# Making the weight sums of a fast-product channel mixer in DRAM with adding transfers

## The chip, the cores and the metric

The kernel runs on one core of one Trainium2 chip. The core has a matrix engine (TensorE, "PE" in the profile; its weight loads are "PEld"), three engines for element work (VectorE "DVE", ScalarE "ACT", GpSimd "POOL") and SyncE ("SP"), which in this kernel only issues transfers. Sixteen DMA engines move the data. The metric is the device time of one execution in microseconds, the median of several runs.

## The reference: what is computed

The program is a small decoder trunk on 512 positions of width 1024, in float32: two layers, each a channel mixer, a token mixer and a second channel mixer, and a last norm. The first layer's token mixer is a latent attention (MLA), the second's a sparse attention (NSA). Only the channel mixers matter here:

```python
def swiglu(x, w_gate, w_up, w_down):
    return (jax.nn.silu(x @ w_gate) * (x @ w_up)) @ w_down

for i in range(DEPTH):
    h = h + 0.5 * swiglu(rmsnorm(h, ffn_norm_a[i]), ffn_a_w_gate[i], ffn_a_w_up[i], ffn_a_w_down[i])
    h = h + mixer_i(rmsnorm(h, mix_norm[i]))
    h = h + 0.5 * swiglu(rmsnorm(h, ffn_norm_b[i]), ffn_b_w_gate[i], ffn_b_w_up[i], ffn_b_w_down[i])
```

The hidden width is 2816, which is 22 blocks of 128. There are four channel mixers in all; in the order of the program they are numbered 1 to 4 here (`idx` 0 to 3 in the code). MLA runs between 1 and 2, NSA between 3 and 4, and 3 follows 2 directly.

## The kernel before, in words

**Tiles.** The residual stream lives in SBUF as eight tiles of 128 channels x 512 positions (`h`). Every operand of a matrix product is split into a high part, rounded to the fast matrix format, and the low remainder (`split`: ACT writes the high part with a copy, DVE subtracts it from the source to get the low part), and each product is done as three matrix instructions: high x high, high x low, low x high.

**A channel mixer** (`ffn`) goes through 22 hidden blocks `f`. For the first three (`PLAIN = 3`) gate and up products are done directly (`plain`). For `f` = 3 to 21 the two products, which share their input, are done as a 2x2 block product with seven products in place of eight (`product(j, ...)`, j = 1 to 7). The seven left operands come from the four quarters g0, g1 (gate weights, two halves of the input channels) and u0, u1 (up weights): g0, g1, u1 unchanged, and the four sums s1 = u0 + u1, u0 + g0, g0 + s1 and g1 + g0 + s1. `wsums` loads the gate slab (`rg`, tile tag `wr`, 512 KB) and the up slab (`ru`, 512 KB) on SP's queue, makes the four sums on DVE in place, and splits all seven operands on ACT and DVE. The 12 matrix instructions of one product take about 1.36 us, and the products of a block run in the order 1, 7, 6, 2, 5, 4, 3. Products 1, 6 and 5 add up in one PSUM bank (`x`, tile `px`), 7 and 4 in another (`q`, tile `pq`); between them ACT copies the bank out (lines 554, 556, 558, 561). So product 5 may only start when the copy of line 558 is done, and that copy waits for product 6; only product 2 lies between.

**Down products** lag behind: after the seven products of block `f` stand two or three `unit`s, each 18 matrix instructions for one 128-channel piece of the output over three finished hidden blocks. A unit loads its weights (`wdr`, 192 KB, two buffers) on SP's queue, ACT and DVE split them (`wd`), and DVE adds the result to `h` (line 468).

**What sets the order.** The program is written as above, and a scheduler that works with modelled costs then decides the order of the instructions on each engine and of the transfers on SP's queue. Each engine takes its own instructions in that order and waits at the head when an operand is not there; so does SP with the transfers it issues, and their data then goes through one queue, `q1`. Loads run far ahead of use where buffers allow: the up slab has three buffers and is loaded about two and a half blocks before its products, the gate slab two buffers, the unit weights two. POOL takes part only at the norms (line 289, sums of squares) and in the token mixers.

Of the kernel before, what the change touches and what calls it, by code (L numbers as in the profile page):

```python
# [11 lines left out]
F32 = mybir.dt.float32  # L12
# [3 lines left out]
ALU = mybir.AluOpType  # L16
# [30 lines left out]
HS = S // 2  # L47
KP = KC // 2
PLAIN = 3
PAD = 16  # L50
TILES = 24
XC = P + 2
# [9 lines left out]
class Kern:  # L62
# [13 lines left out]
    def setup(self):  # L76
        nc, cp, a = self.nc, self.cp, self.a

        self.nw, self.odd, self.nq = 0, 0, 0
        self.first = self.wp.tile([P, 2048 + 3 * PAD], F32R, tag="w0", name="w")
        small = self.wp.tile([P, 80], F32, name="small")
        self.vtc_all = small
        self.vtc, self.small_sums, self.stc = small[:, :12], small[:, 12:16], small[:, 32:]
        self.sts, self.nst = [small[:, 12 + 3 * i : 15 + 3 * i] for i in range(6)], 0
        self.gains = cp.tile([P, 64], F32, name="gains")
        nc.scalar.dma_start(self.gains[:, :53], a["gains"])
        self.ident = cp.tile([P, P], F32, name="ident")
        nc.scalar.dma_start(self.ident, a["c_ident"])  # L90
        self.ones = cp.tile([P, P], F32R, name="ones")
        nc.vector.memset(f32v(self.ones), 1.0)
        warm = self.bank("o", "warm")
        for _ in range(10):
            nc.tensor.matmul(warm.rearrange("p (a n) -> p a n", n=P), self.ones, self.ones[:, None, :].to_broadcast([P, 4, P]), start=True, stop=True)
        nc.scalar.dma_start(self.gains[:, 53:59], a["c_rvalid"])
        tiny = self.gains[:, 59:64]
        nc.scalar.activation(tiny[:, 0:1], f32v(self.ones)[:, 0:1], AF.Copy)
        self.tiny = tiny

        self.ngains = cp.tile([P, 32], F32, name="ngains")
        for i, x in enumerate(FGAINS):
            nc.vector.tensor_scalar(self.ngains[:, 8 * i : 8 * i + 8], self.gains[:, GAINS[x] : GAINS[x] + 8], -1.0, None, op0=ALU.mult)
        self.h, self.ahead, self.softmax, self.turn, self.chain, self.chained, self.hi_pool = [], [], False, 0, None, False, False
        self.gated = None
        self.h = [self.hp.tile([P, S], F32, name=f"h{c}") for c in range(KC)]

    def begin(self):
# [232 lines left out]
    def wsums(self, idx, f):  # L341


        nc, fp, w_gu = self.nc, self.fp, self.a["w_gu"]
        if f == PLAIN:

            rg = fp.tile([P, 1024], F32, tag="fr", bufs=3, name="rg")
        else:
            rg = self.wp.tile([P, 1024], F32, tag="wr", bufs=2, name="wr")
        nc.sync.dma_start(rg, w_gu[idx, f, 0])  # L350
        ru = fp.tile([P, 1024], F32, tag="fr", bufs=3, name="ru")
        nc.sync.dma_start(ru, w_gu[idx, f, 1])
        s1 = fp.tile([P, S], F32, tag="s1", bufs=1, name="s1")
        g0, g1, u0, u1 = rg[:, :S], rg[:, S:], ru[:, :S], ru[:, S:]

        def split(src, pool, tag, bufs):
            n = src.shape[1]
            if pool is self.wp:
                hi, lo = self.wtiles("half")
            elif n == 1024:  # L360
                hi, lo = self.sum_tiles(n)
            else:
                hi = pool.tile([P, n], F32R, tag=tag[0], bufs=bufs, name="wh")
                lo = pool.tile([P, n + 2 * PAD], F32R, tag=tag[1], bufs=bufs, name="wl")[:, 2 * PAD :]
            with self.tc.issue_after(self.evicted.ins) if f == PLAIN + 1 else nullcontext():
                self.split(src, hi, lo)
            return [(hi[:, x : x + S].rearrange("p (k c) -> p k c", c=P), lo[:, x : x + S].rearrange("p (k c) -> p k c", c=P))
                    for x in range(0, n, S)]

        w = {}  # L370
        w[1], w[2] = split(rg, self.wp, None, 2)
        nc.vector.tensor_tensor(s1, u0, u1, op=ALU.add)
        nc.vector.tensor_tensor(u0, u0, g0, op=ALU.add)
        w[7], w[4] = split(ru, fp, ("fh", "fl"), 3)
        nc.vector.tensor_tensor(g0, g0, s1, op=ALU.add)
        nc.vector.tensor_tensor(g1, g1, g0, op=ALU.add)
        w[6], w[3] = split(rg, fp, ("fh", "fl"), 3)
        w[5], = split(s1, fp, ("sh", "sl"), 2)
        return w
# [36 lines left out]
    def third_slab(self, src):  # L416
# [4 lines left out]
            self.split(raw, *w)  # L421
        self.ahead.append([t.rearrange("p (a b) -> p a b", b=P) for t in w])

    def pad(self, pool, n, tag):
        pool.tile([P, n], F32, tag=tag, bufs=1, name=tag)

    def ffn(self, idx, gain_next, ap, tp):
        nc, a = self.nc, self.a
        self.scr, self.fp = (tp, "sq", 1), tp
        ah, al, ht, row = {}, {}, [], None  # L430
        self.pad(ap, 5 * PAD, "pad0")
        tg, tu, units = {}, {}, []
# [34 lines left out]
        def add(c, p):  # L467
            nc.vector.scalar_tensor_tensor(self.h[c], p, 0.5, self.h[c], op0=ALU.mult, op1=ALU.add)  # L468
# [72 lines left out]
        for f in range(PLAIN, NF):  # L541
# [25 lines left out]
            for work, tag in zip(todo, "oTS"):  # L567
                work(tag)
            act(f)
        if gain_next == "fin":  # L570

            hs, out = [self.parts(self.four(F32)) for _ in range(4)], []
# [961 lines left out]
```

## Time and profile before

| what | value |
|---|---|
| median of 3 runs | 1863.67 us (1863.41 to 1864.48) |
| the profiled execution's own time | 1862.05 us |
| its span, first to last instruction | 1860.3 us |
| granted TensorE clock | 0.999 |
| PE busy | 1845.7 us, 99% |
| PEld busy | 1763.4 us, 95% |
| DVE, ACT, POOL busy | 81%, 57%, 16% |
| DMA | 196.64 MB, mean 106 GB/s over the span |
| HBM read, written | 178.44 MB, 2.16 MB |

The page gives busy time for each engine, a strip of 40 slices, the DMA queues, the chain of work that ended last, the costliest groups of instructions, and the issues of transfers with the time from issue to landing. Matrix instructions are pipelined: one of 256 columns is listed with 276 ns, but in an undisturbed stretch the next starts 0.11 us later, so a short stall hides in the overlap and shows only in the distance between starts. A row of the timeline gives the start, the duration, the engine and line, the operation with its tiles, and in brackets how long the engine had stood idle and what ended that.

### The profile page before, as it was taken

The page shows a single profiled execution, that of the slowest core. Times are in us where ns is not written, and L with a number is a line of the kernel's source. Part 1 is how long each engine was busy: PE and PEld are TensorE (multiplying, and loading weights), DVE is VectorE, ACT ScalarE, POOL GpSimd, SP SyncE. Part 2 cuts the span into 40 slices and gives each one's busy share as a digit, 9 for nine tenths or more (in the row PEclk, how much of TensorE's full clock was granted, in tenths as well). Part 3 has the DMA queues.
Part 4 walks back from the last instruction along what each step waited for, and adds up shares of the span by engine and source line. Part 5 has one row for each costly group of instructions (what it writes and reads, how often), then busy time and mean ns, then how long its engine had stood idle before and what let it go on. Part 6 is the DMA issues. An engine that isn't in the chain of part 4 may idle for free.

```text
span 1860.3 us, 37031 instructions
## 1 busy us (share of the span) xinstructions
PE 1845.7 (99%) x14464; PEld 1763.4 (95%) x14464; DVE 1507.4 (81%) x2810; ACT 1064.5 (57%) x1997; POOL 296.7 (16%) x370
## 2 busy tenths in 40 slices
PE   9999999999999999999999999999999999999998
PEld 9999999888889999999999999988888889999997
DVE  8988886688779988886898888666878888888885
ACT  7555553567666555554655545446776865555554
POOL 0000000258830000001000000022666620000000
PEclk9999999999999999999999999999999999999999
DMA  6433331434433433322443332162433133433321
GB/s 238 132 108 103 103 92 48 117 105 103 114 123 112 119 103 109 110 73 72 138 118 110 109 106 81 45 183 82 108 108 103 40 118 116 121 104 107 103 78 69
DMA packets 84351, 196.64 MB, mean 106 GB/s; under 512 B 10944, under 2 KB 38464, under 8 KB 84176
## 3 DMA queue, kind: packets, MB, share of 16 engines
q1 hardware_dynamic: 81664, 191.34, 34.9%
q10 hardware_dynamic: 2512, 2.93, 0.5%
q8 instruction: 114, 1.87, 0.4%
q14 instruction: 61, 0.50, 0.1%
HBM read 178.44 MB, written 2.16 MB: 97 GB/s over the span
## 4 chain that ended last, share of the span: by engine, by line
PE 93%; DVE 3%; ACT 1%; issue 1%; POOL 1%; DMA 0%; ACTq 0%; POOLq 0%; DVEq 0%
PE pd L462 8%; PE pd L464 8%; PE pd L463 8%; PE px L386 6%; PE px L388 6%; PE px L387 5%; PE pg L386 4%; PE pg L388 4%; PE pg L387 4%; PE pq L386 4%; PE pq L388 4%; PE pq L387 4%; PE o L1337 2%; PE pt L1310 2%; PE po L197 2%; PE po L199 2%
## 5 line engine op out<-in xcount | busy, mean ns | idle before, releaser
L462 PE MATMUL pd<-ah,wd 128*128 128x256 f32 x1152 | 318.3, 276 | 0.0
L464 PE MATMUL pd<-ah,wd 128*128 128x256 f32 x1152 | 318.3, 276 | 0.0
L463 PE MATMUL pd<-al,wd 128*128 128x256 f32 x1152 | 318.3, 276 | 0.0
L289 POOL TENSOR_TENSOR s<-s,sq 128x512 f32<-128x512 f32 x38 | 54.7, 1441 | 1050.3 <-ACT sq L285 1050.3
L462 PEld LDWEIGHTS pd<-ah,wd 128*128 128x128 f32 x1152 | 216.3, 188 | 0.0
L464 PEld LDWEIGHTS pd<-ah,wd 128*128 128x128 f32 x1152 | 216.3, 188 | 0.0
L463 PEld LDWEIGHTS pd<-al,wd 128*128 128x128 f32 x1152 | 216.3, 188 | 0.0
L206 DVE TENSOR_TENSOR w<-wr,w 128x1024 fp32r<-128x1024 f32 x72 | 88.2, 1225 | 120.7 <-ACT w L205 120.4
L386 PE MATMUL px<-four,wh 128*128 128x256 f32 x608 | 168.4, 277 | 0.4 <-ACT wh L205 0.2
L388 PE MATMUL px<-four,wl 128*128 128x256 f32 x608 | 168.2, 277 | 0.2 <-DVE wl L206 0.2
L386 PE MATMUL pq<-four,wh 128*128 128x256 f32 x608 | 168.1, 276 | 0.2 <-ACT uq L556 0.2
L387 PE MATMUL px<-four,wh 128*128 128x256 f32 x608 | 168.0, 276 | 0.0
L388 PE MATMUL pq<-four,wl 128*128 128x256 f32 x608 | 167.9, 276 | 0.0
L387 PE MATMUL pq<-four,wh 128*128 128x256 f32 x608 | 167.9, 276 | 0.0
L468 DVE SCALAR_TENSOR_TENSOR h<-pd,h 128x512 f32<-128x512 f32 x216 | 148.3, 686 | 15.4 <-PE pd L464 15.2
L205 ACT ACTIVATE wd<-wdr 128x384 fp32r<-128x384 f32 x192 | 99.2, 519 | 103.8 <-issue 64.6
L176 ACT ACTIVATE w<-wr 128x1024 fp32r<-128x1024 f32 (+3 forms) x89 | 80.8, 908 | 87.5 <-PE pd L464 20.6
L206 DVE TENSOR_TENSOR wd<-wdr,wd 128x384 fp32r<-128x384 f32 x192 | 105.8, 553 | 20.1 <-ACT wd L205 20.0
L178 DVE TENSOR_TENSOR w<-wr,w 128x1024 fp32r<-128x1024 f32 (+3 forms) x75 | 78.3, 1044 | 50.0 <-ACT w L176 49.8
L728 ACT ACTIVATE p<-p,small 128x512 f32<-128x512 f32 (+2 forms) x192 | 106.9, 558 | 19.0 <-DVE small L727 15.3
L386 PEld LDWEIGHTS px<-four,wh 128*128 128x128 f32 x608 | 114.1, 188 | 1.0 <-ACT wh L205 0.4
L388 PEld LDWEIGHTS px<-four,wl 128*128 128x128 f32 x608 | 114.2, 188 | 0.6 <-DVE wl L206 0.6
(379 smaller groups left out, 6264.9 us busy)
## 6 DMA issues: line engine op xcount, KB each, us to landing
wr<-in_w_gu SPq DMA_DIRECT2D x93, 512.0 KB, 3.5
ru<-in_w_gu SPq DMA_DIRECT2D x76, 512.0 KB, 4.3
wdr<-in_w_down SPq DMA_DIRECT2D x192, 192.0 KB, 2.5
wr<-in_w_down SPq DMA_DIRECT2D x24, 256.0 KB, 2.6
wr<-in_mla_w_o SPq DMA_DIRECT2D x8, 512.0 KB, 3.4
th<-btab_d SPq DMA_DIRECT2D x16, 256.0 KB, 3.7
wr<-in_nsa_w_q SPq DMA_DIRECT2D x8, 512.0 KB, 3.8
wr<-in_nsa_w_o SPq DMA_DIRECT2D x8, 512.0 KB, 3.7
```

The lines of the kernel that those rows point to most:

```text
L176: self.copied = nc.scalar.activation(wh[:, m], raw[:, m], AF.Copy)
L178: nc.vector.tensor_tensor(wl[:, m], raw[:, m], f32v(wh[:, m]), op=ALU.subtract)
L205: nc.scalar.activation(hi, src, AF.Copy)
L206: (nc.gpsimd if pool else nc.vector).tensor_tensor(lo, src, f32v(hi), op=ALU.subtract)
L386: mm(out, wh[:, p], xh, start=first and p == 0, stop=False, skip_group_check=True)
L387: mm(out, wh[:, p], xl, start=False, stop=False, skip_group_check=True)
L388: mm(out, wl[:, p], xh, start=False, stop=last and p == KP - 1, skip_group_check=True)
L462: nc.tensor.matmul(o, wh, xh, start=k == b0 and x == 0, stop=False, skip_group_check=True)
L463: nc.tensor.matmul(o, wh, xl, start=False, stop=False, skip_group_check=True)
L464: last = nc.tensor.matmul(o, wl, xh, start=False, stop=k == b1 - 1, skip_group_check=True)
L468: nc.vector.scalar_tensor_tensor(self.h[c], p, 0.5, self.h[c], op0=ALU.mult, op1=ALU.add)
L728: nc.scalar.activation(p_sb[:, :n], p_sb[:, :n], AF.Exp, bias=nm, scale=-1.0, accum_out=sm)
```

## The change

For channel mixers 2, 3 and 4 the four sums of the blocks `f` = 3, 4, 5 and 6 are no longer made by DVE in those blocks. They are made in DRAM while the channel mixer before (1, 2 or 3) is running. For each such block a DRAM tile of 128 x 2560 floats is filled: SP issues one copy from DRAM to DRAM of both slabs (1,024 KB) and one of the second half of the up slab (256 KB), and POOL then issues four transfers of 256 KB each that add what they bring to what stands at the destination: u0 onto u1 (gives s1), g0 onto u0, s1 onto g0, and that sum onto g1. The third and fourth wait for the ones before them. The SP copies are tied to come after the load of the up slab of `f` = 9, 10, 11 or 12 of the running mixer.

In the block itself SP then loads, beside the plain gate slab, three pieces out of the DRAM tile: 512 KB into `ru` (as many bytes as before), 256 KB into `s1`, and 512 KB into a new tile `rp` with two buffers. The DVE sums fall away there; the splits stay. Mixer 1 and the blocks from 7 on are as before. The sums themselves are the same.

```diff
+SUMS = 3, 4, 5, 6
...
     def wsums(self, idx, f):
...
         nc.sync.dma_start(rg, w_gu[idx, f, 0])
         ru = fp.tile([P, 1024], F32, tag="fr", bufs=3, name="ru")
-        nc.sync.dma_start(ru, w_gu[idx, f, 1])
+        made = self.sums.pop((idx, f), None)
+        self.loaded = nc.sync.dma_start(ru, w_gu[idx, f, 1] if made is None else made[:, 1024:2048])
         s1 = fp.tile([P, S], F32, tag="s1", bufs=1, name="s1")
+        if made is not None:
+            rs = self.ap.tile([P, 1024], F32, tag="rp", bufs=2, name="rp")
+            nc.sync.dma_start(s1, made[:, 2048:])
+            nc.sync.dma_start(rs, made[:, :1024])
...
         w[1], w[2] = split(rg, self.wp, None, 2)
+        if made is not None:
+            w[7], w[4] = split(ru, fp, ("fh", "fl"), 3)
+            w[6], w[3] = split(rs, fp, ("fh", "fl"), 3)
+            w[5], = split(s1, fp, ("sh", "sl"), 2)
+            return w
         nc.vector.tensor_tensor(s1, u0, u1, op=ALU.add)
         nc.vector.tensor_tensor(u0, u0, g0, op=ALU.add)
         w[7], w[4] = split(ru, fp, ("fh", "fl"), 3)
         nc.vector.tensor_tensor(g0, g0, s1, op=ALU.add)
         nc.vector.tensor_tensor(g1, g1, g0, op=ALU.add)
...
+    def add_up(self, idx, f):
+
+        nc, src = self.nc, self.a["w_gu"][idx, f]
+        t = self.sums[idx, f] = self.dp.tile([P, 5 * S], F32, name=f"sums{idx}{f}")
+        with self.tc.issue_after(self.loaded.ins):
+            nc.sync.dma_start(t[:, :2048].rearrange("p (z n) -> p z n", z=2), src.rearrange("z p n -> p z n"))
+            nc.sync.dma_start(t[:, 2048:], src[1, :, S:])
+        add = partial(nc.gpsimd.dma_start, accum_op=ALU.add)
+        add(t[:, 2048:], src[1, :, :S])
+        add(t[:, 1024 : 1024 + S], src[0, :, :S])
+        add(t[:, :S], t[:, 2048:])
+        add(t[:, S:1024], t[:, :S])
...
     def ffn(self, idx, gain_next, ap, tp):
...
+        early = [partial(self.add_up, idx + 1, x) for x in SUMS] if idx < 3 else []
...
             act(f)
+            if early and f >= 3 * NG:
+                early.pop(0)()
```

**First place: SP's queue in mixer 2, around the start of its hidden block 7.** `wr` and `ru` are slabs of later blocks, `wdr` the weights of the block's units. Before:

```order
L350 DMA wr<-in_w_gu 128x1024
L352 DMA ru<-in_w_gu 128x1024
L474 DMA wdr<-in_w_down 128x384 x3
L350 DMA wr<-in_w_gu 128x1024
L352 DMA ru<-in_w_gu 128x1024
```

and now, with the DRAM tile of mixer 3's block 5 (`sums`):

```order
L351 DMA wr<-in_w_gu 128x1024
L354 DMA ru<-in_w_gu 128x1024
L440 DMA sums_9181<-in_w_gu 128x2x1024
L501 DMA wdr<-in_w_down 128x384 x2
L441 DMA sums_9181<-in_w_gu 128x512
L501 DMA wdr<-in_w_down 128x384
L351 DMA wr<-in_w_gu 128x1024
L354 DMA ru<-in_w_gu 128x1024
```

The 1,024 KB copy stands between the up slab and the first unit weights of the block, the 256 KB copy between the second and the third. In mixers 1, 2 and 3 together twelve such pairs are in the queue.

**Second place: ACT in the same block.** `wd<-wdr` is the split of the first unit weights, the other rows are the copies out of PSUM and the split of the next gate slab. Before:

```order
L554 ACTIVATE pg<-px 128x256
L205 ACTIVATE wd<-wdr 128x384
L556 ACTIVATE uq<-pq 128x256
L558 ACTIVATE uq<-px 128x256
L205 ACTIVATE w<-wr 128x1024
```

and now:

```order
L581 ACTIVATE pg<-px 128x256
L583 ACTIVATE uq<-pq 128x256
L206 ACTIVATE wd<-wdr 128x384
L585 ACTIVATE uq<-px 128x256
L206 ACTIVATE w<-wr 128x1024
```

The split of the unit weights has gone behind the first copy of `pq`, and still stands ahead of the second copy of `px`.

**Third place: SP's queue in mixer 2 while its blocks 3 to 5 run.** Here the made sums of mixer 2 are loaded: `ru` and `rp` of 512 KB, `s` of 256 KB. Now:

```order
L354 DMA ru<-sums_2588 128x1024
L501 DMA wdr<-in_w_down 128x384 x2
L351 DMA wr<-in_w_gu 128x1024 x2
L354 DMA ru<-in_w_gu 128x1024
L359 DMA rp<-sums_2588 128x1024
L358 DMA s_7809<-sums_2375 128x512
L501 DMA wdr<-in_w_down 128x384 x2
L354 DMA ru<-in_w_gu 128x1024
L358 DMA s_7988<-sums_2588 128x512
L501 DMA wdr<-in_w_down 128x384
```

Before, this stretch held `wr`, `wdr` and `ru` alone. `s` has one buffer, so the load of `s_7988`, which is the sum s1 of block 6, follows the split of block 5's, and it stands behind two unit weights and an up slab.

More of the change, by code (lines that the diff above doesn't have):

```diff
@@ L104, in setup @@
         self.h, self.ahead, self.softmax, self.turn, self.chain, self.chained, self.hi_pool = [], [], False, 0, None, False, False
-        self.gated = None
+        self.gated, self.sums = None, {}
         self.h = [self.hp.tile([P, S], F32, name=f"h{c}") for c in range(KC)]
@@ L428, in ffn @@
         nc, a = self.nc, self.a
-        self.scr, self.fp = (tp, "sq", 1), tp
+        self.scr, self.fp, self.ap = (tp, "sq", 1), tp, ap
+        early = [partial(self.add_up, idx + 1, x) for x in SUMS] if idx < 3 else []
+        if not idx:
+            ap.tile([P, 1024], F32, tag="rp", bufs=2, name="rp")
         ah, al, ht, row = {}, {}, [], None
```

## The prediction

> **What bounds the kernel now.** I read the page's first part, then the stages (the windows), then the waits around one block.
>
> ```profile
> PE 1845.7 (99%) x14464; PEld 1763.4 (95%) x14464; DVE 1507.4 (81%) x2810; ACT 1064.5 (57%) x1997; POOL 296.7 (16%) x370
> ...
> q1 hardware_dynamic: 81664, 191.34, 34.9%
> ...
> wr<-in_w_gu SPq DMA_DIRECT2D x93, 512.0 KB, 3.5
> ru<-in_w_gu SPq DMA_DIRECT2D x76, 512.0 KB, 4.3
> wdr<-in_w_down SPq DMA_DIRECT2D x192, 192.0 KB, 2.5
> ```
>
> PE is busy 99% of the span, so work taken from DVE is worth only the time in which PE waits for DVE or for ACT behind it. Both sides of the sum follow from that: how much PE waits in the blocks that lose their DVE sums, and whether the new transfers make PE wait where it does not now. The windows show blocks 3 to 6 of mixer 2 and 3 to 5 of mixers 3 and 4, cut at the first product of each block, and for comparison two later blocks (two columns of times are enough: length, then PE busy).
>
> ```profile
> 580.20:596.10 15.90, 15.89 (x140) 15.70 (x139) 13.04 (x20) 9.56 (x15) 0.00 (x0) 1.00 0.31 92
> 596.10:611.90 15.80, 15.80 (x141) 15.78 (x140) 15.61 (x24) 8.89 (x16) 0.00 (x0) 1.00 0.47 138
> 611.90:625.50 13.60, 13.60 (x123) 13.60 (x122) 13.56 (x22) 6.86 (x12) 0.00 (x0) 1.00 0.39 108
> 625.50:641.10 15.60, 15.60 (x140) 15.60 (x139) 13.95 (x23) 8.51 (x14) 0.00 (x0) 1.00 0.42 126
> 641.10:656.80 15.70, 15.70 (x141) 15.70 (x140) 12.92 (x21) 7.85 (x13) 0.00 (x0) 1.00 0.36 108
> 915.70:931.80 16.10, 15.99 (x141) 15.79 (x140) 12.54 (x19) 9.59 (x15) 0.00 (x0) 1.00 0.22 66
> 931.80:948.10 16.30, 15.96 (x141) 15.77 (x140) 15.59 (x25) 8.80 (x16) 0.00 (x0) 1.00 0.46 134
> 1547.60:1563.80 16.20, 15.96 (x141) 15.77 (x140) 13.34 (x20) 9.61 (x15) 0.00 (x0) 1.00 0.31 91
> 1563.80:1579.90 16.10, 16.10 (x140) 15.98 (x139) 15.81 (x25) 9.01 (x16) 0.00 (x0) 1.00 0.47 136
> ```
>
> A block with three units takes 15.6 to 15.7 us when nothing is late (fourth and fifth row). Blocks 3 and 4 of the three mixers take 15.9, 15.8, 16.1, 16.3, 16.2 and 16.1, together 96.4; six times 15.65 is 93.9. The block of two units (13.6, third row) is already as short as its like elsewhere, though DVE is busy 13.56 of 13.60 in it. **So all that making the sums elsewhere can win in these blocks is 2.5 us, 0.13% of the run.** The change of DVE's load is far larger (four sums in each of twelve blocks, 33 us by 0.69 us each), but PE does not wait for it.
>
> ```profile
> L372 DVE TENSOR_TENSOR s<-ru x76: 680/687/696, 29.0 to 1790.2; 128x512 f32<-128x512 f32 x76
> ```
>
> **The change part by part.**
>
> *Removed:* 48 DVE sums, worth the 2.5 us.
>
> *Added loads in blocks 3 to 6.* Per block 768 KB more on SP's queue. The DMA share in these stages is 0.22 to 0.47, so the bytes fit. The place to look at is `s`, with its single buffer: the load of block 6's s1 can only be issued when DVE has split block 5's, early in block 4, and it stands behind two unit weights and an up slab. I take the issue at about 4.3 us into block 4 and 1,152 KB to pass by then; at the queue's fastest (430 GB/s, below) that is 2.7 us, so it lands about 8.3 us into the block. ACT wants to split `s` at 6.9 us (648.02 against a start of 641.13 in the rows below), and the copy of line 561 stands behind it. That copy must be done before product 3, six products or 8.2 us into the block. ACT would then end about 1 us too late: between 0 and 2, I take 1, in three mixers: +3.0. With the 2.5 won, the blocks whose sums are made cost +0.5 (from -2.5 to +3.5).
>
> *Added copies.* They run where PE has no slack to speak of. These are SP's issues, ACT's rows and three of PE's in block 7 of mixer 2 (start, duration, what ended the idle time), and the strip of what the DMA engines moved in that block, in slices of 0.4 us:
>
> ```profile
> 636.49 0.33 SPq L350 DMA_DIRECT2D wr<-in_w_gu  x1
> 638.22 0.33 SPq L352 DMA_DIRECT2D ru<-in_w_gu  x1
> 641.09 4.31 SPq L474 DMA_DIRECT2D wdr<-in_w_down  x3
> ...
> 642.69 0.37 ACT L554 ACTIVATE pg<-px 128x256 f32<-128x256 f32 x1 [2.03 <-PE px L388]
> 643.93 0.53 ACT L205 ACTIVATE wd<-wdr 128x384 fp32r<-128x384 f32 x1 [0.87 <-DMA wdr<-in_w_down]
> 644.36 0.37 ACT L556 ACTIVATE uq<-pq 128x256 f32<-128x256 f32 x1
> 645.41 0.38 ACT L558 ACTIVATE uq<-px 128x256 f32<-128x256 f32 x1 [0.69 <-PE px L388]
> 648.02 0.63 ACT L205 ACTIVATE wh<-s 128x512 fp32r<-128x512 f32 x1 [0.18 <-PE px L387]
> ...
> 641.13 0.28 PE L386 MATMUL px<-x,w 128*128 128x256 f32 x1
> 645.22 0.28 PE L386 MATMUL pg<-x,w 128*128 128x256 f32 x1
> 646.58 0.28 PE L386 MATMUL px<-four,wh 128*128 128x256 f32 x1
> ...
> GB/s 307 184 119 114 277 108 142 261 65 0 0 0 31 192 261 8 41 0 0 0 0 0 0 0 0 0 0 0 0 0 205 61 256 430 348 72 113 133 328 420
> ```
>
> ACT already stands waiting for the landing of the first unit weights (0.87 us). Behind that split is the copy of line 558, and product 5 (646.58) cannot start before it. The slack of the landing is the idle time before line 558 (0.69), plus 646.58 less the copy's end at 645.79, less some 0.07 for the signal (0.72), plus 0.37 because the change puts the copy of line 556 ahead of the split: 1.8 us. The same stands at seven more starts of blocks where a copy now lies ahead of a unit weight for which ACT waits. Their rows of line 558 (the first has no idle time left: it ran 0.49 late, so its slack is 0.6):
>
> ```profile
> 108.87 0.38 ACT L558 ACTIVATE uq<-px 128x256 f32<-128x256 f32 x1
> 124.02 0.38 ACT L558 ACTIVATE uq<-px 128x256 f32<-128x256 f32 x1 [0.37 <-PE px L388]
> 616.17 0.38 ACT L558 ACTIVATE uq<-px 128x256 f32<-128x256 f32 x1 [0.46 <-PE px L388]
> 661.05 0.38 ACT L558 ACTIVATE uq<-px 128x256 f32<-128x256 f32 x1 [0.92 <-PE px L388]
> 952.34 0.38 ACT L558 ACTIVATE uq<-px 128x256 f32<-128x256 f32 x1 [0.40 <-PE px L388]
> 981.58 0.38 ACT L558 ACTIVATE uq<-px 128x256 f32<-128x256 f32 x1 [0.84 <-PE px L388]
> 997.22 0.38 ACT L558 ACTIVATE uq<-px 128x256 f32<-128x256 f32 x1 [0.91 <-PE px L388]
> ```
>
> The eight slacks, each idle time plus 1.09, add up to 12.8 us. The other four of the twelve copies lie ahead of unit weights whose landing ACT does not wait for; I cost them at nothing, covered by the other splits that ACT does first, and without that cover at the same lateness as the eight.
>
> How late does the landing get? The up slab ahead lands 4.3 us after its issue; the copy's 1,024 KB (1.05 MB) pass next and take C; 192 KB at 430 GB/s take 0.5. So the unit weights land 4.8 + C after the up slab's issue. Now they land 2.87 (641.09 - 638.22) + about 2.6 = 5.5 after it. The lateness is C - 0.7. For C no row exists, since nothing here goes from DRAM to DRAM. Below: 430 GB/s, the highest slice of the strip, 2.4 us. Above: half that pace, as DRAM is both read and written, 4.9 us. I take the queue's own mean pace, 191.34 MB in 34.9% of 1860.3 us or 295 GB/s, so C = 3.6: its packets are of the same kind as the copies'. Lateness 2.9, eight times 23.2, less 12.8 of slack: **+10.4 us**. The ends: 1.7 late passes the slack only at four starts, together +1.7; 4.2 late gives 33.6 - 12.8 = +20.8.
>
> The Trainium skill, "DMA: Bandwidth & Descriptors", section "Latency and other measured facts", gives 207 to 214 GB/s in each direction for copies between HBM tensors; by it C is an estimated 4.9 us, my upper end, and the copies would cost 20.8. No run here shows it.
>
> *Added adding transfers.* 48, each 256 KB brought to a destination that is itself read and written: 0.6 us of the 16 engines at 430 GB/s, up to 1.8 if all three streams count. They come in POOL's own queue, so a unit weight shares the engines with them rather than standing behind them. Four in a block of 15.6 fill 16 to 46% of the time; of the 5 us between the up slab's issue and the unit weights' landing that is 0.8 to 2.3 us if they fall there. Six of the eight starts follow an earlier copy and can meet them; half of them or less will. I take 0.4 each, +2.4 (0 to 9). POOL itself is covered: it waits 1050.3 us for ACT's squares, and its issues stand there. The sums are ready in time: mixer 2 starts them in its blocks 5 to 8 (611.90 and on) for mixer 3's blocks from 915.70 on, and the other pairs lie farther apart, with a token mixer between.
>
> ```profile
> POOL s L289 <- ACT sq L285: 1050.3, 37, 329.6
> ```
>
> *Sum:* 0.5 + 10.4 + 2.4 = +13.3 us on the profiled execution's 1862.05, that is 1875.4. The median of the runs lies 1.6 above that execution, so **1877 us**.
>
> **The rivals.**
>
> *Hidden transfers (the other side: not slower).* The DMA engines idle two thirds of the time. If a copy passes at 430 GB/s and the adds are through before the next block, the copies cost 1.7, and with -2.5 to +1 in the made blocks the time is 1862.9 to 1866.4, no change. It decides at C = 2.5 us or less. For it: single slices reach that pace. Against: two streams meet DRAM.
>
> *The DMA engines become the bound.* Loads of 1.6 MB, copies of 1.25 MB, adds of 1 MB counted three times make 5.9 MB in 15.6 us, 375 GB/s, near the strip's highest slice. The lateness then grows from copy to copy and reaches 6 us: 48 - 12.8 = +35, time 1899. For it: nothing in the page has run that dense for long. Against: the adds can spread into the ten blocks behind.
>
> *Faster.* Even all 2.5 us and a perfect cover give 1861.2, inside no change. For more, the waits ahead of block 3 (the three direct blocks) would have to shrink too: PE's list of waits has only this for all of them:
>
> ```profile
> PE pg L402 <- DVE x L209: 0.2, 1, 0.2
> ```
>
> *The change does nothing it says* (sums late, loads wait for them): excluded by the distances above.
>
> **How the numbers follow.** A measurement of this kernel can tell about 0.2%, 3.7 us, from no change: the band is 1859.9 to 1867.4. Forecast case (some copies felt, 1867.4 to 1886): 0.47. Hidden transfers: 0.28. DMA as the bound (beyond 1886): 0.21. Faster: 0.04. The likeliest case's own range is 1868 to 1886. For 8 in 10 the range starts at 1862, where the hidden case's lower end lies, and ends at 1895, the forecast's upper ends (20.8 + 9 + 2 over 1863.7) and part of the dense case.
>
> **What would show it right or wrong.** Right: ACT's wait for `wdr` (34.8 us in all now) grows by some 20 to 25 us; the gaps before product 5 in blocks 5, 7 and 8 of mixers 2 and 3 and 7 and 8 of mixer 1, and nowhere after block 10; a copy's landing at 6 to 8 us from issue; blocks 3 and 4 of mixers 2 to 4 at 15.65. Wrong: copies that land in under 5 us with block starts as before; or ACT's splits of `s` setting gaps larger than 1 us, which would move the cause from the copies to the loads.
>
> ```profile
> ACT wd L205 <- DMA wdr<-in_w_down: 34.8, 39, 2.2
> ```

## The result, and the profile after

| | before | after |
|---|---|---|
| median of the runs, us | 1863.85 (1863.41 to 1864.48, 4 runs) | 1882.88 (1876.44 to 1886.72, 4 runs) |
| the profiled execution's own time, us | 1862.05 | 1881.65 |
| its span, us | 1860.3 | 1879.5 |

The change makes the kernel slower, by a factor of 1.010 (95% interval 1.0084 to 1.0116), 19 us. The prediction was 1877 us with a range of 1862 to 1895: right in sign, 6 us short in size. It is 13.3 us of slowdown predicted in the profiled execution against 19.6 found there.

These are lines of the page of the kernel after: busy time, and the issues of transfers with the median time from issue to landing.

```profile
PE 1849.9 (98%) x14464; PEld 1766.1 (94%) x14464; DVE 1478.2 (79%) x2762; ACT 1064.2 (57%) x1997; POOL 337.4 (18%) x418
...
wdr<-in_w_down SPq DMA_DIRECT2D x192, 192.0 KB, 2.7
...
sums<-in_w_gu SPq DMA_DIRECT2D x12, 1024.0 KB, 7.4
sums<-in_w_gu POOLq DMA_DIRECT2D x24, 256.0 KB, 6.0
sums<-sums POOLq DMA_DIRECT2D x24, 256.0 KB, 5.3
```

DVE has lost its sums (29 us less work), PE has the same number of instructions, and still 19 us came on top. The windows of the kernel after, cut at the first product of each block, say where. In order they are blocks 7 and 8 of mixer 1, blocks 3, 4, 5, 7 and 8 of mixer 2, blocks 4, 7 and 8 of mixer 3, and block 4 of mixer 4 (blocks 3 of mixers 3 and 4 read as that of mixer 2). The first number behind the limits is the length, the last two are the DMA share and GB/s.

```profile
104.50:122.70 18.20, 15.87 (x140) 15.67 (x139) 13.32 (x21) 7.69 (x13) 4.44 (x7) 1.00 0.86 247
122.70:141.30 18.60, 15.58 (x123) 15.38 (x123) 11.30 (x18) 6.57 (x11) 4.74 (x6) 0.91 0.75 197
588.60:604.20 15.60, 15.60 (x140) 15.60 (x139) 10.19 (x14) 9.73 (x15) 0.00 (x0) 1.00 0.48 156
604.20:622.00 17.80, 16.58 (x141) 16.19 (x140) 14.17 (x23) 8.21 (x14) 0.00 (x0) 1.00 0.56 173
622.00:635.60 13.60, 13.60 (x123) 13.60 (x122) 9.21 (x15) 6.81 (x11) 2.51 (x3) 1.00 0.71 169
651.20:668.40 17.20, 15.95 (x140) 15.76 (x139) 13.36 (x21) 7.68 (x13) 4.17 (x5) 1.00 0.91 251
668.40:684.70 16.30, 14.25 (x123) 14.05 (x122) 11.33 (x18) 6.66 (x11) 3.31 (x4) 1.00 0.85 221
945.60:963.10 17.50, 16.18 (x140) 15.79 (x139) 13.78 (x22) 8.28 (x14) 0.00 (x0) 1.00 0.57 179
992.40:1009.50 17.10, 15.99 (x141) 15.79 (x140) 13.39 (x21) 7.67 (x13) 4.16 (x5) 1.00 0.90 251
1009.50:1025.10 15.60, 13.88 (x123) 13.69 (x122) 10.99 (x18) 6.58 (x11) 3.34 (x4) 1.00 0.88 228
1581.90:1599.10 17.20, 16.12 (x140) 15.91 (x140) 13.84 (x22) 8.28 (x14) 0.00 (x0) 1.00 0.54 169
```

An undisturbed block takes 15.6 (three units) or 13.6 (two). Blocks 7 and 8 of mixers 1 to 3, where the copies and the adding transfers run, are too long by 2.6, 5.0, 1.6, 2.7, 1.5 and 2.0, together 15.4 us. Blocks 3 of mixers 2 to 4 are at 15.6, so the gain there is real; blocks 4 are at 17.8, 17.5 and 17.2. The six together are 99.3 against 96.4 before: +2.9. That makes 18.3 of the 19.2 by which the span grew; the rest lies in differences of 0.1 to 0.2 in other places. Block 5 of mixer 2 begins behind the first copy, and its first adding transfer is issued only at 625.57, after its first unit weights have landed (625.38): it is at its 13.6.

The waits of PE and of ACT name the two mechanisms. Line 585 is the copy of product 6 out of PSUM (558 before), line 588 that of product 5 (561 before).

```profile
PE px L397 <- ACT uq L585: 11.5, 6, 3.0
PE pg L397 <- ACT pg L588: 3.6, 3, 1.3
...
ACT wd L206 <- DMA wdr<-in_w_down: 49.7, 38, 4.4
...
ACT wh L206 <- DMA s<-sums: 9.7, 6, 2.2
```

Six waits before product 5, three before product 3; behind the first stands ACT's wait for unit weights, behind the second its wait for `s`. How it looks at the worst place, the start of block 8 of mixer 1, the timeline shows (SP's issues of the up slab, of the 1,024 KB copy and of the unit weights, two of POOL's three issues, ACT's rows and product 5):

```profile
119.51 0.33 SPq L354 DMA_DIRECT2D ru<-in_w_gu  x1
119.89 0.59 SPq L440 DMA_DIRECT2D sums<-in_w_gu  x1
122.38 1.44 SPq L501 DMA_DIRECT2D wdr<-in_w_down  x2
...
121.57 0.84 POOL L446 DMA_DIRECT2D sums<-sums  x1 [3.88 <-DMA sums<-sums]
122.17 1.09 POOL L444 DMA_DIRECT2D sums<-in_w_gu  x1
...
130.53 0.52 ACT L206 ACTIVATE wd<-wdr 128x384 fp32r<-128x384 f32 x1 [4.42 <-DMA wdr<-in_w_down]
130.96 0.36 ACT L585 ACTIVATE uq<-px 128x256 f32<-128x256 f32 x1
131.38 0.38 PE L397 MATMUL px<-four,wh 128*128 128x256 f32 x1 [3.02 <-ACT uq L585]
```

And the strips of the DMA engines' busy tenths and of GB/s from 119.5 to 134.0, in slices of 0.36 us:

```profile
DMA  9999999989977999999999999999999985327660
GB/s 192 198 316 441 407 396 384 350 350 316 328 294 271 384 418 362 345 326 270 325 226 247 232 232 253 237 259 229 261 250 261 280 236 154 96 62 100 234 237 30
```

The unit weights are issued at 122.38 and ACT can start on them at 130.53; the same load before landed 3.1 us after its issue. Ahead of it pass the up slab and the 1,024 KB copy, at 270 to 440 GB/s, up to about 127. From then on, to 131, the pace is only 226 to 280 GB/s (each byte counted once) although the engines are full. In that time the unit weights and the adding transfers share them. The packets in the trace between 127.0 and 130.0, counted by queue:

```
queue          packet   count   median duration
q1 (SP)        1.5 KB     197     79 ns    unit weights
q0 (POOL)      2.0 KB     199    176 ns    adding transfers
```

In this stretch there is one packet of the one for one of the other. A unit weight of 192 KB has 128 packets, on average 8 on each of 16 engines. An estimate from the table's durations is 0.6 us for them alone and 8 x (79 + 176) ns = 2.0 us in turns, and two such loads stand in the queue.

### The profile page after: what moved, and what is told of

It is laid out like the page before. It is cut to its first block, busy times and chain, and to the rows that moved or that the text cites. A ratio compares the mean times of both kernels' runs of the same rounds, so it can differ in the third digit from the quotient of the medians.

```text
span 1879.5 us, 37151 instructions
## 1 busy us (share of the span) xinstructions
PE 1849.9 (98%) x14464; PEld 1766.1 (94%) x14464; DVE 1478.2 (79%) x2762; ACT 1064.2 (57%) x1997; POOL 337.4 (18%) x418
## 4 chain that ended last, share of the span: by engine, by line
PE 85%; DVE 6%; DMA 4%; ACT 2%; issue 1%; POOL 1%; SPq 0%; ACTq 0%; DVEq 0%; POOLq 0%
PE pd L489 7%; PE pd L490 7%; PE pd L491 7%; PE px L397 5%; PE px L398 5%; PE px L399 5%; PE pg L397 3%; PE pg L398 3%; PE pg L399 3%; PE pq L397 3%; PE pq L399 3%; PE pq L398 3%; DMA wdr<-in_w_down 2%; PE o L1366 2%; DVE wl L207 2%; PE pt L1339 2%
## 5 line engine op out<-in xcount | busy, mean ns | idle before, releaser
L397 PE MATMUL px<-four,wh 128*128 128x256 f32 x608 | 170.0, 280 | 11.8 <-ACT uq L585 11.5
L206 ACT ACTIVATE wd<-wdr 128x384 fp32r<-128x384 f32 x192 | 99.3, 519 | 125.4 <-issue 69.3
L397 PEld LDWEIGHTS px<-four,wh 128*128 128x128 f32 x608 | 114.5, 188 | 14.0 <-ACT uq L585 13.3
L397 PEld LDWEIGHTS pq<-four,wh 128*128 128x128 f32 x608 | 114.7, 189 | 0.4 <-ACT uq L583 0.4
```

What stands on the lines that cost most here:

```text
L206: nc.scalar.activation(hi, src, AF.Copy)
L397: mm(out, wh[:, p], xh, start=first and p == 0, stop=False, skip_group_check=True)
```

## The experiments

The theories. **A**, the prediction's: the copies, ahead of the unit weights in SP's queue, make them late; the adds matter little. **B**: the adding transfers make them late by sharing the engines. **C**: it takes both at the same place. **D**, formed later: an adding transfer costs time where it is in flight when a block's first unit weights are loaded, and nothing elsewhere. Ratios are to the kernel before, run on the same chip, with 95% intervals.

### The copies without the adds

```diff
-        add(t[:, 2048:], src[1, :, :S])
-        add(t[:, 1024 : 1024 + S], src[0, :, :S])
-        add(t[:, :S], t[:, 2048:])
-        add(t[:, S:1024], t[:, :S])
```

> The 48 adding transfers on POOL's queue are left out (so the sums are not made: the DRAM tiles hold the plain weights); the 12 pairs of copies on SP's queue and all loads stay where the change has them. The changed kernel takes 1882.9 us. Theory A, as predicted: the copies that stand ahead of the unit weights in SP's queue are most of the cost (10.4 of the predicted 13.3 us), the adds little. Then the stalls at block starts of 14.8 us in the changed trace fall by a few us only: 1875 to 1880 us. Theory B, from the changed trace: at the first copy of mixers 2 and 3, which no add accompanies, no stall is seen, so the adds, which share the DMA engines packet by packet, make most of it. Then the copies alone cost 0 to 2 us and the time is 1866 to 1869 us.

Measured: 1866.69 us (1865.10 to 1867.76), ratio 1.0016 (1.0006 to 1.0025). Its waits before products 3 and 5:

```profile
PE pg L397 <- ACT pg L584: 2.1, 3, 1.0
PE px L397 <- ACT uq L581: 1.5, 2, 1.3
```

The strip of the transfers around block 8 of mixer 1 (119 to 126, slices of 0.175 us):

```profile
GB/s 421 421 398 117 47 211 47 117 117 94 234 374 421 421 421 398 421 398 398 421 398 421 421 374 398 421 398 445 445 439 354 389 313 389 380 345 278 301 322 351
```

With all twelve pairs of copies in their place, product 5 waits at two starts instead of six, for 1.5 us instead of 11.5. The copy passes at 398 to 421 GB/s, the pace of a load. Theory A falls: 16.2 of the 19 us (1882.88 - 1866.69) need the adding transfers.

### The loads alone

```diff
-        made = self.sums.pop((idx, f), None)
-        self.loaded = nc.sync.dma_start(ru, w_gu[idx, f, 1] if made is None else made[:, 1024:2048])
+        made = True if idx and f in SUMS else None
+        self.loaded = nc.sync.dma_start(ru, w_gu[idx, f, 1])
...
-            nc.sync.dma_start(s1, made[:, 2048:])
-            nc.sync.dma_start(rs, made[:, :1024])
+            nc.sync.dma_start(s1, w_gu[idx, f, 1][:, S:])
+            nc.sync.dma_start(rs, w_gu[idx, f, 0])
...
-        early = [partial(self.add_up, idx + 1, x) for x in SUMS] if idx < 3 else []
+        early = []
```

> No copies and no adds; the blocks 3 to 6 of mixers 2 to 4 load the same number of bytes as in the changed kernel, but straight from the weights in DRAM, so these operands are plain weights and not their sums. Both theories: the block starts of 15.6 us come back, blocks 3 stay at 15.64, and the wait for s in block 4 stays (+5.0, less the 2.5 us won): 1866 to 1867.5 us. If the time is above 1870, the loads and not the making of the sums carry part of what I put down to copies and adds; if it is 1864 or less, the wait for s came from traffic of the copies.

Measured: 1865.29 us (1864.16 to 1866.86), ratio 1.0007 (0.9998 to 1.0017), 0.7 below the range expected. A row of its waits:

```profile
PE pg L397 <- ACT pg L588: 2.8, 3, 1.4
```

The three waits for `s` before product 3 are there without any copy or add, so they belong to the loads in the mixers that use the sums. What they cost eats the gain of the missing DVE sums: the kernel is where it was before, or 1.6 us above. Against this one, the copies alone cost 1.4 us.

### The copies behind the unit weights

```diff
-        with self.tc.issue_after(self.loaded.ins):
+        with self.tc.issue_after(self.unit_load.ins):
...
-            nc.sync.dma_start(raw, a["w_down"][idx, c, :, b0 * P : (b0 + NG) * P])
+            self.unit_load = nc.sync.dma_start(raw, a["w_down"][idx, c, :, b0 * P : (b0 + NG) * P])
```

> The copies are tied behind the last unit weights of a block in place of behind the up slab, so that the first unit weights of a block, for which ACT waits, have no copy ahead of them; the adds follow the copies as before. Theory A (place in the queue): the stalls go almost all, 1867 to 1870 us. Theory B (the adds share the engines): the adds still run across the block starts, and more than half of the 14.8 us stays: 1872 to 1880 us.

Measured: 1867.14 us (1864.89 to 1870.93), ratio 1.0021 (1.0011 to 1.0030). All transfers are there, and 15.7 of the 19 us are gone: the copies leave the queue ahead of the first unit weights, and the adds, which follow the copies, move with them to another part of the block. Read alone this run would speak for theory A, and the first for theory B. Together they exclude both as they stand: without adds +1.4 over the loads alone, with adds but the copies behind +1.9, with both in the places of the change +17.6. The wide spread of the runs suggests that where the adds fall is left to chance here; that is not shown.

### A second buffer for `s`

```diff
-        s1 = fp.tile([P, S], F32, tag="s1", bufs=1, name="s1")
+        s1 = fp.tile([P, S], F32, tag="s1", bufs=2, name="s1")
```

> A second buffer for s, nothing else. If the single buffer makes the load of block 6's s late, block 4 of mixers 2 to 4 goes from 17.5 to 15.64 us (5.0 us in all): 1876 to 1879 us. If instead the place of that load behind two unit weights and an up slab makes it late, the buffer changes nothing: 1881 to 1885 us.

Measured: 1879.92 us (1878.98 to 1880.69), ratio 1.0087 (1.0072 to 1.0102). In its waits of PE the row of the copy before product 3 is gone, and the other stays:

```profile
PE px L397 <- ACT uq L585: 12.5, 6, 4.3
```

So the single buffer makes these waits: blocks 4 go from 17.8, 17.5 and 17.2 to 15.6, 15.6 and 15.8, which gives back 5.5 us, close to the 5.0 expected. The time falls by only 3.0 (1882.88 - 1879.92), 0.9 short of the range, because the waits before product 5, and the half clock behind them (last section), came out larger: in the two profiled executions, blocks 7 and 8 of mixer 1 take 41.0 us here and 36.8 after the change.

### The adds away from the copies

The copies stay where the change puts them; the four adds of a block are tied behind a hidden block 13 to 16, where no copy runs.

```diff
+    def adds(self, idx, f, gate):
+        nc, src, t = self.nc, self.a["w_gu"][idx, f], self.sums[idx, f]
+        held = self.small_gate[:, :1]
+        held = nc.gpsimd.tensor_tensor(held, gate[:, :1], gate[:, :1], op=ALU.add)
         add = partial(nc.gpsimd.dma_start, accum_op=ALU.add)
+        with self.tc.issue_after(held.ins):
...
+            if idx < 3 and 13 <= f < 13 + len(SUMS):
+                self.adds(idx + 1, SUMS[f - 13], f32v(al[f]))
```

> The copies stay where the change has them. The adds of the four blocks are held back by a one-column operation on POOL that needs the low part of hidden block 13, 14, 15 and 16, so they run, four at a time, across the starts of blocks 14 to 17, with no copy near. Copies without adds cost 2.0 us of stalls (e1), the loads 1.4 us (e2). Theory C: it takes both, a copy ahead in the queue and adds that take turns with it. Then the adds by themselves cost under 1.5 us: 1866.5 to 1868.5 us. Theory D: the adds slow the unit weights by themselves. Then the starts of blocks 14 to 17 stall: 1872 to 1880 us.

Measured: 1868.81 us (1868.22 to 1871.40), ratio 1.0029 (1.0020 to 1.0039). This is near the range of theory C (0.3 above it) and far from that of D. But the timeline shows that the adds had not only been parted from the copies. At the start of block 14 of mixer 1 POOL issued them 1.05 us behind the first unit weights (its row, then SP's and ACT's):

```profile
212.90 1.02 POOL L451 DMA_DIRECT2D sums<-in_w_gu  x1
...
211.85 4.01 SPq L509 DMA_DIRECT2D wdr<-in_w_down  x3
...
214.39 0.53 ACT L207 ACTIVATE wd<-wdr 128x384 fp32r<-128x384 f32 x1 [0.56 <-DMA wdr<-in_w_down]
```

The weights landed 2.5 us after their issue, as if nothing were beside them. At four other starts, with no copy in flight, 102 to 213 adding packets do pass before the first unit weights land; these take 4.1 to 4.9 us, and product 5 waits at two of the four, for 0.3 and 0.45 us. That is D's mechanism, small enough to be covered. By its time alone this run cannot tell C from D.

### Plain transfers in place of adding ones

```diff
-        add = partial(nc.gpsimd.dma_start, accum_op=ALU.add)
+        add = nc.gpsimd.dma_start
```

> The 48 transfers on POOL's queue keep their place, their waits and their bytes, but write plainly and do not add (the sums are not made). In the changed trace an adding packet of 2 KB holds an engine about 178 ns, where a plain packet of 2 KB from SBUF to DRAM took 84 ns. Theory C1: the time that an adding packet holds the engine is the price. Then the stalls fall from 14.8 us to 6 or less: 1868 to 1873 us. Theory C2: that a second queue takes every other turn is the price, whatever its packets take. Then they stay above 10 us: 1877 to 1884 us.

Measured: 1877.31 us (1873.27 to 1879.70), ratio 1.0071 (1.0057 to 1.0085). The wait before product 5 is a little over half of that after the change:

```profile
PE px L397 <- ACT uq L585: 6.6, 7, 2.6
```

POOL's transfers land in 3.4 and 4.0 us instead of 6.0 and 5.3:

```profile
sums<-in_w_gu POOLq DMA_DIRECT2D x24, 256.0 KB, 3.4
sums<-sums POOLq DMA_DIRECT2D x24, 256.0 KB, 4.0
```

By the medians 5.6 us of the 19 go with the adding (1882.88 - 1877.31), and 13.6 remain with plain transfers in POOL's queue at that place. The size of the split is uncertain: the two sets of four runs overlap (the other is 1876.44 to 1886.72), and the profiled execution here is the fastest of its four. Neither theory is met whole: the time lies in the range of C2, the 6.6 us of waits between the two. Nor did the edit change the kind of packet alone: the plain transfers go as 3,072 packets of 4 KB at 159 ns, where the adding ones go as 6,144 of 2 KB at 178 ns (medians of the two traces).

### Copies behind, two buffers

The edits of the third and the fourth experiment together.

> The copies behind the last unit weights of a block (e3, 3.6 us of stalls left where adds meet block starts) and a second buffer for s (no wait in block 4). The 2.5 us won in blocks 3 and 4 then stand against 3.6: 1863.7 - 2.5 + 3.6 = 1864.8, from 1863.5 to 1866 us. All theories expect this; above 1867 the price of the loads is not the s buffer.

Measured: 1863.75 us (1861.21 to 1868.02, 10 runs), ratio 1.0001 (0.9992 to 1.0010): no change from the kernel before. The savings of the two edits add up: by the medians the buffer gives 1867.14 - 1863.75 = 3.4 here and 3.0 above.

### Paced adds, tied to the block's end

Only blocks 3 and 4 are made in DRAM; copies behind the unit weights, two buffers for `s`, and one step of the adds in each block, tied behind `tu`.

```diff
-SUMS = 3, 4, 5, 6
+SUMS = 3, 4
...
+            if idx < 3 and f > 3 * NG:
+                due = [(SUMS[x], f - 3 * NG - 1 - x) for x in range(len(SUMS)) if 0 <= f - 3 * NG - 1 - x < 3]
+                if due:
+                    held = nc.gpsimd.tensor_tensor(self.small_gate[:, :1], t[:, HS : HS + 1], t[:, HS : HS + 1], op=ALU.add)
+                    with self.tc.issue_after(held.ins):
+                        for x, step in due[::-1]:
+                            self.adds(idx + 1, x, step)
```

> The version that the runs so far point to: sums in DRAM for blocks 3 and 4 alone, which are the ones where PE waits before; copies behind the last unit weights; the adds one step per block, each held back by a one-column operation on POOL until 6.8 us into a block, so that they are through before the next block's start; two buffers for s. Theory C and the account of the waits: no stall is left, the 2.5 us are won: 1861 to 1862.5 us against 1863.7. If blocks 5 and 6 need DVE's relief too, or adds still meet block starts, 1863 to 1866 us.

Measured: 1873.27 us (1870.11 to 1876.12), ratio 1.0050 (1.0037 to 1.0062), some 11 us above what was expected. `tu` is multiplied in place at the end of the block, and the tie took the last writer. So each step was issued just ahead of the next block's unit weights, here by 0.43 us; this is the start of block 14 of mixer 1, with one add of 256 KB in flight and no copy near:

```profile
211.09 0.84 POOL L454 DMA_DIRECT2D sums<-sums  x1 [0.32 <-issue]
...
211.52 7.35 SPq L509 DMA_DIRECT2D wdr<-in_w_down  x3
...
217.40 0.52 ACT L207 ACTIVATE wd<-wdr 128x384 fp32r<-128x384 f32 x1 [3.58 <-DMA wdr<-in_w_down]
```

All its waits before product 5:

```profile
PE px L398 <- ACT uq L593: 9.7, 8, 2.2
```

The weights landed 5.8 us after their issue. The miss is the best evidence of the study: half the adds, no copy in flight at any of the eight late starts, and the waits before product 5 are nearly those of the change. It does not take both, so theory C falls. D also says why the fifth experiment lost little (1868.81 against 1866.69 with the copies alone), and why the third did: with the copies the adds had moved behind the first unit weights (in block 8 of mixer 1 they were issued from 130.02 on, the weights at 119.71).

### The same adds, some 5 us into the block

One edit to the kernel before: the tie is to the copy of product 6 out of PSUM, and stands right behind it.

```diff
+                    held = nc.gpsimd.tensor_tensor(self.small_gate[:, :1], uq[:, HS : HS + 1], uq[:, HS : HS + 1], op=ALU.add)
```

> This is the paced kernel before it with one edit: what POOL's transfers are tied behind is the copy of product 6 out of PSUM, about 4.4 us into a block, in place of the block's end. Blocks 3 and 4 of mixers 2 to 4 are made in DRAM, s has two buffers, the copies are tied behind the last unit weights. Theory D (an adding transfer costs time only where it is in flight when the first unit weights of a block are loaded): all stalls before product 5 are gone, the first unit weights land 2.4 us after their issue throughout, 2.4 us is won in blocks 3 and 4, and the time is 1861 to 1863. Rival E (adding transfers delay whatever unit weights run beside them, and the later ones stop PE as the first did): again some 10 us of stalls, 1870 to 1876 as in the paced kernel before. Between: the second or third unit weights come late but are covered, 1863 to 1866.

Measured: 1861.99 us (1860.89 to 1863.37, 11 runs), ratio 0.9990 (0.9982 to 0.9999). The same add, the same load of unit weights of block 14, and ACT's row:

```profile
199.55 0.84 POOL L454 DMA_DIRECT2D sums<-sums  x1 [0.32 <-issue]
...
209.82 4.27 SPq L509 DMA_DIRECT2D wdr<-in_w_down  x3
...
212.29 0.53 ACT L207 ACTIVATE wd<-wdr 128x384 fp32r<-128x384 f32 x1 [0.50 <-DMA wdr<-in_w_down]
```

2.4 us from issue to landing instead of 5.8, and no wait before product 5 is left in the list. The same transfers in the same number: 11.3 us (1873.27 - 1861.99) for the place in the block. Theory D holds. Against the kernel before, 1.7 us are won of the 2.4 expected.

### The whole change, with its transfers in the quiet part

As before, with `SUMS = 3, 4, 5, 6`, so everything that the change makes in DRAM.

> As the kernel sent with it, for blocks 3 to 6 (all that the change makes in DRAM): up to four adding transfers in a block, 1 MB, some 5 to 6 us from 4.4 us on, so through by about 11 us, ahead of the next block's unit weights at 13.6 or 15.6. Theory D: 1861 to 1863.5, with stalls of less than 1 us in each mixer. Rival E: twice the adds of the other kernel, so 1875 to 1885.

Measured: 1861.23 us (1860.19 to 1862.09, 11 runs), ratio 0.9987 (0.9978 to 0.9996): 2.5 us faster than the kernel before on the same chip (1863.71), the whole of what blocks 3 and 4 had to give. Three of POOL's four issues in a block whose first unit weights were issued at 193.67:

```profile
199.17 0.81 POOL L449 DMA_DIRECT2D sums<-in_w_gu  x1 [0.40 <-issue]
199.72 1.11 POOL L450 DMA_DIRECT2D sums<-in_w_gu  x1
...
203.85 0.82 POOL L454 DMA_DIRECT2D sums<-sums  x1 [2.16 <-issue]
```

The waits of ACT for unit weights, and all that PE waits for ACT in the products:

```profile
ACT wd L207 <- DMA wdr<-in_w_down: 49.7, 38, 2.7
...
PE pq L398 <- ACT uq L591: 0.2, 1, 0.2
```

ACT waits 49.7 us for unit weights, to the tenth what it waited after the change, and in the list PE waits for none of it. The longest single wait is 2.7 instead of 4.4: it is the single landing against its slack that counts, not the sum. The margin is thin. Other than expected, the adds are not all through at the next start: at thirteen starts one or more are still in flight, with at most 27 packets to go, and the first unit weights take 3.2 to 5.0 us. At the start of block 14 of mixer 1 they take 4.55, and that block lasts 14.0 instead of 13.6.

## Why the prediction was right, and where not

**The gain available: right.** 2.5 us in blocks 3 and 4. After the change blocks 3 had their part; the tenth experiment, by its median, has all of it.

**The wait for `s`: right place and mechanism, size short.** The term was 1 us in each of three mixers, +3.0, and the sum over the made blocks +0.5. Found: blocks 4 at 17.8, 17.5 and 17.2 against 15.6, 5.7 us, and the made blocks at +2.9; with the second buffer blocks 4 give back 5.5. The landing was forecast well: in block 4 of mixer 2 the load of `s` is issued 4.5 us into the block and lands at 8.8, where 4.3 and 8.3 were forecast. But the forecast's own terms, 4.3 and 2.7, make 7.0; the 1.3 us up to 8.3 have no row behind them, and the trace shows 4.3 us from issue to landing. The prediction's sign that a wait for `s` above 1 us would move the cause from the copies to the loads was wrong: the waits were up to 1.3 us and still a sixth of the loss.

**The copies: right places in the main, wrong price.** Six of the eight named starts are late, and none after block 10 by more than 0.2 us; the first copies of mixers 2 and 3, at the starts of block 5, cost nothing. The term was +10.4 from C = 3.6 us for 1,024 KB. The copy runs at 398 to 421 GB/s, C = 2.6 us; with that, the prediction's own formula (lateness C - 0.7 = 1.9, over the eight slacks) gives 2.6. The first experiment has 1.4 in time, and at the start with the least slack 1.35 us of wait, where the formula gives 1.3. The median landing of 7.4 us, inside the 6 to 8 that were to show the term right, counts the up slab ahead and the adds beside (6.3 without the adds), so it did not test C. The Trainium skill, "DMA: Bandwidth & Descriptors", section "Latency and other measured facts", gives 207 and 214 GB/s in each direction for copies between HBM tensors in rows of 16 KiB, at the two row pitches that ran best; the prediction's estimate from it was 20.8 us for the copies. The strip of the first experiment does not agree: 398 to 421 GB/s, in packets of 4 KB.

**The adding transfers: this is the step that failed.** "I take 0.4 each, +2.4 (0 to 9)": found is 1882.88 - 1866.69 = 16.2 us, beyond the upper end. The prediction counted the time that the adds' bytes take on the engines (0.6 to 1.8 us for 256 KB; the packets' 8 x 178 ns = 1.4 us lie within) and spread it over the block. But what counts is how late the first unit weights land beside them: one add in flight made them 3.4 us late (5.8 instead of 2.4, eighth and ninth experiment), where the forecast's slacks are 0.6 to 2.0. And six starts met adds, not half of them or less: the third and fourth add of a block wait for the ones before, so that a chain of four takes longer than a block (in mixer 2 one runs from 642.92 to 663.21), and an add is in flight at the next start. So the forecast's 13.3 came out near 19 with its two large terms the wrong way round: the copies' term was 8 to 9 too large, the adds' 14 too small. A third loss, the half clock described in the last section, was not in the sum at all. That the time fell within 6 us of the forecast is luck: two errors of opposite sign.

**The rivals.** Hidden transfers, set to decide at C of 2.5 us or less with the adds through before the next block, was nearly right on the copies and failed on the adds. The DMA engines as the bound: they are 0.85 to 0.91 busy in five of the six late blocks and the lateness does grow from block 7 to block 8, as that rival had it. The 221 to 251 GB/s of these five rows count each byte once; counted as the rival counts, the adds three times, they come to 349 to 373, near its 375. So the engines were about as full as it said, with the adds' packets taking 41 to 46% of their busy time. It failed on the size: the first unit weights land 5.0 us later than before at the worst start (8.1 after their issue, 3.1 before), not 6 at all eight, and the ten blocks behind are free of it. The last experiment moves the same bytes without the loss, so it is the place of the adds and not the load of the engines that costs. Faster was out of reach for this version, and 1861.2, the figure given there for a perfect cover, is what the tenth experiment measured.

**The signs.** ACT's wait for `wdr` rose by 14.9 us, predicted 20 to 25. The last experiment shows that the sign was not a good one: the same sum stands in a kernel that is faster than before.

## What to carry to other kernels

Moving work off an engine that hides behind another wins only the waits that it causes; here the 29 us by which DVE's busy time fell were worth 2.5. Price an added transfer by what it does to the next load that something waits for (its place in the queue, the packets it takes turns with, the slack of that landing) rather than by its bytes. And when background transfers are free to start at any time, tie them to an event that lies behind the critical load: the transfers of this change cost 17.6 us where it put them (1882.88 - 1865.29) and nothing that the time shows 5 us into a block, and half of the adds cost 11 us just ahead of a block's end.

## What the runs showed of the hardware that was not expected

An adding packet of 2 KB takes 178 ns (median of the 6,144 after the change), a plain one of 2 KB on SP's queue 84 ns. In the worst stretch after the change the two queues shared the engines packet for packet: 197 of 1.5 KB against 199 of 2 KB in 3 us. It is not always so, and the packets' own durations do not explain all: one add of 256 KB, on average 1.4 us on each engine, made unit weights 3.4 us late. In that stretch of the eighth experiment, from 213.75 to 214.75, 76 adding packets stand against 18 of the loads and take 89% of the engines' time; and from 216.25 to 217.40, just before the landing, the engines are on average only 9% busy, so that the load waits for a few last packets. Why the load got so few packets at first, and why its last ones came so late, the traces don't tell, as they don't name a packet's engine. It stays open.

A long stall also costs clock. These are windows of the kernel after (the stall before product 5 in block 8 of mixer 1, and what follows it) and of the kernel with two buffers for `s` (block 7 of mixer 1); the eighth column is the granted clock.

```profile
128.10:131.30 3.20, 0.25 (x3) 0.05 (x1) 0.21 (x1) 0.77 (x3) 0.00 (x0) 1.00 1.09 253
132.10:135.40 3.30, 3.30 (x18) 3.30 (x17) 2.25 (x3) 1.07 (x3) 0.81 (x1) 0.50 0.28 76
135.50:138.90 3.40, 3.40 (x32) 3.40 (x32) 2.87 (x5) 2.15 (x3) 0.41 (x1) 1.00 0.52 77
```

```profile
109.90:112.50 2.60, 0.32 (x4) 0.13 (x2) 0.32 (x1) 0.88 (x3) 0.00 (x0) 1.00 1.13 242
113.00:116.40 3.40, 3.40 (x18) 3.40 (x17) 2.23 (x3) 1.27 (x3) 0.67 (x1) 0.51 0.53 141
```

After the first of these stalls, 3.0 us in the list of waits, PE starts again at full clock, and 0.7 us later falls to half for 3.4 us: 18 matrix instructions where the next stretch has 32, so some 1.6 us on top of the stall. In the profiled execution this happens once, 1.6 us of its 19.6; the kernel with two buffers met it twice. The four runs after the change have granted clocks of 0.999, 0.998, 0.996 and 0.995 in the order of their times, 1876.44 to 1886.72; 0.004 of 1880 us is an estimated 7.5 of the 10.3 between the first and the last.

Why one stall has it and another of the same length at the same place has not (112.44 after the change, a stall of 2.33; 112.47 with two buffers, one of 2.28) shows when the changes of the clock are compared: within a run they lie whole multiples of 3.41 us apart (in the kernel with two buffers the half clock begins at 113.06 and again at 133.54, six times 3.41). Divided into such windows, the nine stalls of 1.9 us or more that the channel mixers have (after the change, with two buffers, and in the sixth and eighth experiment) fall into two groups. The four with 2.20, 2.28, 2.73 and 3.41 us inside one window are followed by half clock from that window's end. The five whose longest part in one window is 1.28, 1.47, 1.60, 1.70 and 1.86 us are not. The rule rests on these nine cases.

The Trainium skill, "TensorE: Matmul & The Clock Gate", section "What's actually happening", has the clock halved after an idle window of about 3.4 us, with windows that run free of the kernel. The length of the windows and their running free agree with these rows; that 2.2 us of waiting inside one can be enough does not follow from it.
